# The low parts of the weights by a negated rounding on ScalarE and an accumulating DMA, in place of a subtraction on VectorE

## The chip, the cores and the metric

One NeuronCore of a Trainium2 chip. The metric is the device time of one execution in microseconds. The kernel before was run twice: 3788.08 and 3795.57 us, median 3791.82 us.

## The reference

The reference is the forward pass of a small network on 512 tokens of 1024 features in float32. First come two layers; each is a feed-forward block, a mixer and a second feed-forward block, every one followed by a layer norm (`LN(alpha*x + f(x))`). The mixer of the first layer ("even") joins a gated linear recurrence and an mLSTM, that of the second ("odd") an RWKV-7 delta rule and gated linear attention. Behind them stand two more layers with RMS norms, each with three kinds of attention (windowed, dilated, to a memory) merged by gates, and a feed-forward block with a short convolution.

```
def swiglu_ffn(x, wi, wo):
    gate, up = jnp.split(x @ wi, 2, axis=-1)
    return (jax.nn.silu(gate) * up) @ wo
```

Most of the work is products of the activations with weight matrices that are each used once: `wi` is 1024 x 5632, `wo` 2816 x 1024, and there are six such pairs beside the mixers' and attentions' matrices. All of it is float32, and the result must be close to float32.

## The kernel before, in words

Activations lie feature-major: eight tiles of 128 features x 512 tokens. A product in float32 is made of three faster passes in the format float32r, which holds fewer bits of the mantissa. Every operand is split in two, `hi` = the value rounded to float32r, and `lo` = value - hi, and a product is hi*hi + hi*lo + lo*hi (`mm3`, line 404).

Weights come as a stream of *slabs* in the order of their use (`plan_w`, line 331). A slab holds the columns of one output tile, 128 of them in most cases, and up to eight row tiles of 128 rows. On chip it is stored as *tiles* of 128 x 512 float32 (256 KB), four row tiles in each, so a full slab has two tiles. SyncE (SP) loads the raw tiles `wr` (`_dma`, line 336), as far as `raw_bufs` slabs ahead of the splitting. Then `_split_hi` (line 355) makes `wh` on ScalarE by a copy with rounding, and `_split_lo` (line 364) makes `wl` on VectorE as raw minus `wh`. `_split` (line 378) makes the low parts of one slab and the high parts of the next one, if there is room. TensorE reads `wh` twice and `wl` once for each row tile.

How far the splitting runs ahead is set when the program is written out. `slab` (line 389) takes the next slab, splits up to it if need be, and then splits `ahead` more (`split_ahead`, line 348), as long as no more than `hl_bufs` slabs are split and not used up. `gemm_first` (line 555), the first four output tiles after a norm, calls `split_ahead` four times more. `hl_bufs` is 8 for the first blocks, 2 with `raw_bufs` 1 in the odd mixer (HLB, RAWB, line 1129), 10, 4 and 7 in later ones. `ahead` is set by `man` (line 2640) at the start of every block: 1, but 2 for attention and 3 for the odd mixer. The constructor's value (line 239) holds only until the first of these calls. Raw, high and low tiles and most activations share one pool of 90 buffers (`f`, line 316); a buffer is taken again when its last reader is done.

The first four slabs, eight tiles, go another way: `load_start` (line 530) loads and splits them by halves of the features through `split_x`, with VectorE making the low part.

The order on each engine comes from three places. A small model in the kernel (`Sched`, line 71) prices every instruction and interleaves the main stream of products with background tasks (norms, mixers, attention); it notes a `dma_start` as landing 2500 ns after its start. A scheduler below it then orders the instructions of every engine by its own estimate and places the semaphores; in the attention blocks VectorE and ScalarE keep the order as written. After that each engine runs its queue in order and stops at an instruction whose operands are not there.

GpSimd (POOL) issues no DMA in this kernel. It has sums of squares and sums for the norms (`Stats.add`, line 594, and `RX.emit`, line 1933), a few products of the mixers and attentions, and memsets of the border columns of the convolution's tiles. A second loader is ScalarE's queue, for some masks, biases and the output.

Of the kernel before, what the change touches and what calls it, by code (L numbers as in the profile page):

```python
# [12 lines left out]
F32R = mybir.dt.float32r  # L13
AF = mybir.ActivationFunctionType
ALU = mybir.AluOpType
# [27 lines left out]
class Engine:  # L43
    """An engine whose instructions are noted with a rough price, for the order of emission."""
# [17 lines left out]
class Core:  # L62
    """The engines under their usual names."""
# [7 lines left out]
class Sched:  # L71
    """Interleaves emission: a main stream and background generators, by an estimate of when TensorE gets to an
    instruction and of when its operands are there. A generator yields a delay, At(time), a condition, or DONE:
    once all that it emitted in this step has run."""
# [6 lines left out]
    def __init__(self):  # L81
        self.t = 0.0
        self.eng = {"vector": 0.0, "scalar": 0.0, "gpsimd": 0.0, "sync": 0.0}
        self.ready, self.by = {}, {}
        # when the readers of a tile are done; the banks in use with the number of their last reader; free banks
        self.free, self.banks, self.idle, self.seq = {}, {}, [0.0] * 8, 0
        self.step_done = 0.0
        self.table = None
        # tasks: (time, number, rank, generator); of those that are due, the lowest rank goes first
        self.heap = []  # L90
        self.n = 0
        self.blocked = []
        self.busy = False
# [51 lines left out]
    def bank(self, ps):  # L145
        """A bank is taken."""
# [8 lines left out]
    def unbank(self, n):  # L155
        """The n banks read last are free."""
# [4 lines left out]
    def upto(self, *aps):  # L161
        """Runs what is due before these operands are there."""
# [63 lines left out]
class G:  # L226
    """What the parts of the kernel share: engines, pools, constants, the weight stream."""

    def __init__(self, ctx, tc, raw_bufs=3, hl_bufs=8, f_bufs=90, q_bufs=16):
# [9 lines left out]
        self.raw_bufs, self.hl_bufs, self.ahead = raw_bufs, hl_bufs, 1  # L239
        self.wq = []  # L240
        self.wi_dma = self.wi_hi = self.wi_split = self.wi_use = self.wi_done = 0
# [11 lines left out]
        # tri[j, i] = 1 where i >= j  # L253
# [10 lines left out]
    # -- TensorE  # L264
# [29 lines left out]
    def pace(self, engine="vector", lead=2000.0):  # L294
        """When that engine is about to run dry."""
# [5 lines left out]
    def acq(self, n):  # L301
        """For a background generator: waits until n banks are free."""
# [13 lines left out]
    def f(self, name, dt=F32, cols=NT):  # L316
        """A tile of up to 520 columns."""
# [5 lines left out]
    def load(self, dst, src):  # L323
        """A load that is not to start ahead of those emitted before it."""
        self.tc.keep_in_program_order(self.nc.sync.dma_start(dst, src))

    # -- the weight stream: slabs [128, kt, cols], in the order of use
# [3 lines left out]
    def plan_w(self, w, c0, cols, k0, kt):  # L331
        """w: DRAM [K, N]; rows 128*k0 .., kt row tiles."""
# [15 lines left out]
    def split_ahead(self, n=1):  # L348
        """Splits up to n more slabs, as far as there is room for them."""
# [5 lines left out]
    def _split_hi(self):  # L355
        parts = []
        for t in self.whl_t[self.wi_hi]:
            hi = self.f("wh", F32R, t.shape[1])
            self.nc.scalar.activation(hi, t, AF.Copy)
            parts.append((t, hi))  # L360
        self.whl_t[self.wi_hi] = parts
        self.wi_hi += 1

    def _split_lo(self):
# [3 lines left out]
        for raw, hi in self.whl_t[j]:  # L368
            lo = self.f("wl", F32R, raw.shape[1])
            self.nc.vector.tensor_tensor(lo, raw, hi, ALU.subtract)  # L370
# [7 lines left out]
    def _split(self):  # L378
        """The low parts of one slab; the high parts of the next one, if there is room."""
        if self.wi_hi == self.wi_split:  # L380
            self._split_hi()
        if self.wi_hi == self.wi_split + 1 and self.wi_hi < min(len(self.wq), self.wi_done + self.hl_bufs):
            self._split_lo()
            if self.wi_hi < self.wi_dma:
                self._split_hi()
        else:
            self._split_lo()

    def slab(self, ahead=None):
        """The next slab: a list of (hi, lo) by row tile."""  # L390
# [11 lines left out]
    # -- three passes of float32r: hi*hi + hi*lo + lo*hi  # L402
# [7 lines left out]
    def rsqrt(self, v, cols=NT):  # L410
        """1/sqrt(v): the table's value and one Newton step."""
# [9 lines left out]
    def preload(self, func):  # L421
        """Brings a function's table in ahead of its use."""
# [10 lines left out]
    def centred(self, ps, name):  # L433
        """ps [tokens, 4 heads of 128], each head less its mean."""
# [20 lines left out]
class Pipe:  # L455
    """Generators that advance by one stage at a time, the oldest first."""
# [7 lines left out]
    def add(self, gen):  # L464
        """One stage for all, then the first of the new one."""
# [9 lines left out]
class X:  # L475
    """Activations, feature-major: eight tiles [128 features, 512 tokens], each as hi + lo."""
# [10 lines left out]
def load_vectors(g, vecs):  # L487
    """vecs: name -> DRAM AP of n*128 values. Leaves each as columns [128, n] on chip."""
# [38 lines left out]
def load_start(g, x, X0, n=4):  # L527
    """x [512, 1024] to feature-major hi/lo, and the first n slabs, both by halves of the features."""
# [22 lines left out]
    g.wi_dma = g.wi_hi = g.wi_split = n  # L551
# [3 lines left out]
def gemm_first(g, xs, n, by_half=True):  # L555
    """The first n output tiles after a norm: the reduction outermost, by halves of the tokens."""
# [27 lines left out]
class Stats:  # L584
    """Sums over the features, per token."""
# [8 lines left out]
    def add(self, y, c=slice(0, NT), fast=False):  # L594
        """Adds one tile's columns c; fast: VectorE, not GpSimd."""
# [19 lines left out]
    def rstd(self, hf, eps):  # L615
        """Emits the mean (PSUM, all partitions) and 1/sqrt(var + eps) for one half."""
# [2088 lines left out]
```

## Time and profile before

| | |
|---|---|
| runs | 3788.08, 3795.57 us, median 3791.82 |
| profiled execution, span from the first to the last instruction | 3778.3 us, which is 13.5 us under the median of the runs; the time around the span is not given for this execution by itself |
| TensorE, matmul | 3718.2 us busy (98%), 19704 instructions |
| TensorE, weight load (beside the matmuls) | 3014.8 us (80%) |
| VectorE | 2083.9 us (55%) |
| ScalarE | 1472.4 us (39%) |
| GpSimd | 363.3 us (10%) |
| DMA | 331.83 MB, 88 GB/s on average; SP's queue keeps the 16 engines busy for 29.9% |
| mean granted TensorE clock | 0.989 of full speed |

Busy time is the time in which at least one instruction of the engine runs. A mean duration times a count can be more than it, since instructions of one engine overlap at their ends. A row of the waits names the waiting engine and its output, the engine and tile it waited for, the total, the number of waits and the longest. Line 55 is the helper that records each instruction and line 279 the one that issues matmuls, so rows are told apart by their tiles. The DMA share of a stretch is the mean busy share of the 16 DMA engines.

### The profile page before, as it was taken

The numbers are of one execution on the slowest core, as the hardware profiler recorded it, in microseconds if no ns is written. First come the engines' busy times: TensorE is split into PE (matmuls) and PEld (weight loads), VectorE is DVE, ScalarE is ACT, GpSimd is POOL, SyncE is SP. The second block draws the span as 40 slices with busy tenths as digits, with TensorE's granted clock in tenths as the row PEclk, the third lists the DMA queues.
The fourth block names the chain that finished last, engine by engine and source line by source line (L and its number), as shares of the span: only waits on it lengthen the run. The fifth ranks groups of instructions, "written<-read, shape, count | busy, mean of one in ns | idle before, by whom it ended". The sixth has DMA issues, their size and how long they took to land.

```text
span 3778.3 us, 52544 instructions
## 1 busy us (share of the span) xinstructions
PE 3718.2 (98%) x19704; PEld 3014.8 (80%) x19704; DVE 2083.9 (55%) x3891; ACT 1472.4 (39%) x2877; POOL 363.3 (10%) x571
## 2 busy tenths in 40 slices
PE   9999999999999999999999999999999999999999
PEld 7888878888888886677888877788888877788888
DVE  4334968333733378677432554558656745467655
ACT  4223664222422255533332433345334434344433
POOL 0001012000200020012000310022000210121001
PEclk9999999999999999889999999999999999999999
DMA  5332322333233311122333242232333242233331
GB/s 160 98 101 77 86 67 86 99 95 95 80 111 98 99 53 41 39 78 71 106 95 90 77 120 76 75 105 68 101 101 102 68 131 65 81 90 90 89 100 52
DMA packets 615090, 331.83 MB, mean 88 GB/s; under 512 B 25233, under 2 KB 608050, under 8 KB 614834
## 3 DMA queue, kind: packets, MB, share of 16 engines
q1 hardware_dynamic: 612018, 324.81, 29.9%
q10 hardware_dynamic: 2816, 3.64, 0.3%
q8 instruction: 155, 2.54, 0.3%
q14 instruction: 101, 0.83, 0.1%
HBM read 323.65 MB, written 4.74 MB: 87 GB/s over the span
## 4 chain that ended last, share of the span: by engine, by line
PE 90%; DVE 7%; ACT 1%; issue 1%; POOL 0%; DMA 0%; SPq 0%; ACTq 0%; DVEq 0%; POOLq 0%
PE m L279 62%; PE mg L279 5%; PE mh L279 3%; PE mf L279 3%; PE tk L279 3%; PE br L279 2%; DVE wl L55 1%; DVE ln_z L55 1%; DVE rm_t L55 1%; PE naS L279 1%; PE naO L279 1%; DVE x L55 1%; DVE xgl L55 1%; PE dO L279 1%; PE dS L279 1%
## 5 line engine op out<-in xcount | busy, mean ns | idle before, releaser
L55 DVE TENSOR_TENSOR wl<-wr,wh 128x512 fp32r<-128x512 f32 (+2 forms) x1208 | 814.9, 720 | 85.4 <-ACT wh L55 84.7
L55 ACT ACTIVATE wh<-wr 128x512 fp32r<-128x512 f32 (+2 forms) x1208 | 664.5, 606 | 93.2 <-PE m L279 50.5
L279 PE MATMUL m<-xh,wh 128*128 128x512 f32 x1544 | 619.3, 401 | 0.0
L279 PE MATMUL m<-xh,wl 128*128 128x512 f32 x1544 | 610.6, 395 | 0.0
L279 PE MATMUL m<-xl,wh 128*128 128x512 f32 x1544 | 610.2, 395 | 0.0
L279 PE MATMUL m<-xgh,wh 128*128 128x512 f32 x1184 | 475.5, 402 | 0.0
L279 PE MATMUL m<-xgl,wh 128*128 128x512 f32 x1184 | 467.6, 395 | 0.0
L279 PE MATMUL m<-xgh,wl 128*128 128x512 f32 x1184 | 467.2, 395 | 0.0
L55 DVE SCALAR_TENSOR_TENSOR hf<-sg,m 128x512 f32<-128x512 f32 x80 | 55.0, 688 | 575.2 <-PE m L279 565.9
L279 PEld LDWEIGHTS m<-xh,wh 128*128 128x128 f32 x1544 | 290.9, 188 | 74.4 <-issue 7.1
L279 PEld LDWEIGHTS m<-xh,wl 128*128 128x128 f32 x1544 | 291.0, 188 | 69.4 <-issue 0.7
L279 PEld LDWEIGHTS m<-xl,wh 128*128 128x128 f32 x1544 | 291.0, 188 | 67.6 <-issue 1.7
L279 PEld LDWEIGHTS m<-xgh,wh 128*128 128x128 f32 x1184 | 222.3, 188 | 62.8 <-issue 14.5
L279 PEld LDWEIGHTS m<-xgh,wl 128*128 128x128 f32 x1184 | 222.3, 188 | 52.3 <-issue 0.7
L279 PEld LDWEIGHTS m<-xgl,wh 128*128 128x128 f32 x1184 | 222.5, 188 | 49.4 <-issue 1.7
L279 PE MATMUL m<-hh,wh 128*128 128x512 f32 x600 | 236.4, 394 | 0.0
L279 PE MATMUL m<-hl,wh 128*128 128x512 f32 x600 | 236.3, 394 | 0.0
L279 PE MATMUL m<-hh,wl 128*128 128x512 f32 x600 | 236.2, 394 | 0.0
L55 ACT ACTIVATE sg<-m 128x512 f32<-128x512 f32 x80 | 47.8, 597 | 424.4 <-PE m L279 424.4
L55 ACT ACTIVATE hh<-hf 128x512 fp32r<-128x512 f32 x88 | 55.7, 633 | 382.6 <-DVE hf L55 382.6
L55 ACT ACTIVATE uc<-up,vecs 128x512 f32<-128x512 f32 x88 | 71.6, 816 | 203.0 <-DVE up L55 202.9
L55 DVE SCALAR_TENSOR_TENSOR uc<-up,vecs,uc 128x512 f32<-128x512 f32 x176 | 131.3, 748 | 13.2 <-ACT uc L55 7.0
(546 smaller groups left out, 6503.7 us busy)
## 6 DMA issues: line engine op xcount, KB each, us to landing
wr<-in_ffn_wi_dram SPq DMA_DIRECT2D x352, 256.0 KB
wr<-in_w_up_dram SPq DMA_DIRECT2D x176, 256.0 KB
wr<-in_ffn_wo_dram SPq DMA_DIRECT2D x160, 256.0 KB
wr<-in_w_in_dram SPq DMA_DIRECT2D x152, 256.0 KB
wr<-in_w_down_dram SPq DMA_DIRECT2D x80, 256.0 KB
wr<-in_od_w_in_dram SPq DMA_DIRECT2D x50, 256.0 KB
wr<-in_ev_w_in_dram SPq DMA_DIRECT2D x48, 256.0 KB
wr<-in_w_out_dram SPq DMA_DIRECT2D x32, 256.0 KB
```

Of the source, the lines that this page charges most:

```text
L55: r = fn(*a, **kw)
L279: return self.nc.tensor.matmul(out, lhsT, rhs, start=start, stop=stop, **kw)
```

## The change

The low part of a tile is no longer a subtraction on VectorE. ScalarE copies the raw tile with a scale of -1 into the low tile, which rounds it to float32r: it then holds minus the high part. A DMA issued by GpSimd adds the raw tile to it in place, from SBUF to SBUF, which leaves raw - hi. ScalarE then makes the high part as before. Both parts of one slab are made in one step, so the counter `wi_hi` and the look-ahead of the high parts go. The constructor's `ahead` becomes 2; `man` and `load_start`'s splitting stay. Comments and docstrings were taken out too; those lines are not shown.

```diff
-        self.raw_bufs, self.hl_bufs, self.ahead = raw_bufs, hl_bufs, 1
+        self.raw_bufs, self.hl_bufs, self.ahead = raw_bufs, hl_bufs, 2
...
-        self.wi_dma = self.wi_hi = self.wi_split = self.wi_use = self.wi_done = 0
+        self.wi_dma = self.wi_split = self.wi_use = self.wi_done = 0
...
-    def _split_hi(self):
-        parts = []
-        for t in self.whl_t[self.wi_hi]:
-            hi = self.f("wh", F32R, t.shape[1])
-            self.nc.scalar.activation(hi, t, AF.Copy)
-            parts.append((t, hi))
-        self.whl_t[self.wi_hi] = parts
-        self.wi_hi += 1
-
-    def _split_lo(self):
+    def _split(self):
         j = self.wi_split
         cols = self.wq[j][2]
         hl = []
-        for raw, hi in self.whl_t[j]:
-            lo = self.f("wl", F32R, raw.shape[1])
-            self.nc.vector.tensor_tensor(lo, raw, hi, ALU.subtract)
+        for raw in self.whl_t[j]:
+            hi, lo = self.f("wh", F32R, raw.shape[1]), self.f("wl", F32R, raw.shape[1])
+            self.nc.scalar.activation(lo, raw, AF.Copy, scale=-1.0)
+            self.nc.gpsimd.dma_start(lo, raw, accum_op=ALU.add)
+            self.nc.scalar.activation(hi, raw, AF.Copy)
             for k in range(lo.shape[1] // cols):
...
         self.wi_split += 1
         self._dma()
-    def _split(self):
-        if self.wi_hi == self.wi_split:
-            self._split_hi()
-        if self.wi_hi == self.wi_split + 1 and self.wi_hi < min(len(self.wq), self.wi_done + self.hl_bufs):
-            self._split_lo()
-            if self.wi_hi < self.wi_dma:
-                self._split_hi()
-        else:
-            self._split_lo()
...
-    g.wi_dma = g.wi_hi = g.wi_split = n
+    g.wi_dma = g.wi_split = n
```

## Rows read from the trace of the kernel before

**Rows 1.** The page, part 1: span, then busy time of each engine and its instructions.
```profile
span 3778.3 us, 52544 instructions
...
PE 3718.2 (98%) x19704; PEld 3014.8 (80%) x19704; DVE 2083.9 (55%) x3891; ACT 1472.4 (39%) x2877; POOL 363.3 (10%) x571
```
**Rows 2.** The page, part 4: the chain that ended last, share of the span by engine.
```profile
PE 90%; DVE 7%; ACT 1%; issue 1%; POOL 0%; DMA 0%; SPq 0%; ACTq 0%; DVEq 0%; POOLq 0%
```
**Rows 3.** Windows of two feed-forward stretches: length, busy (instructions) by engine, clock, DMA.
```profile
core 0: us, PE busy (x) PEld busy (x) DVE busy (x) ACT busy (x) POOL busy (x), PEclk, DMA share, GB/s
697.00:810.00 113.00, 113.00 (x489) 91.48 (x488) 39.05 (x64) 27.72 (x50) 0.00 (x0) 1.00 0.34 98
860.00:940.00 80.00, 80.00 (x347) 64.77 (x346) 25.89 (x42) 23.73 (x44) 0.00 (x0) 1.00 0.26 76
```
**Rows 4.** Waits of TensorE's matmuls over the span: us in total, times, longest.
```profile
PE mf L279 <- DVE xgl L55: 9.6, 10, 1.7
...
PE mk L279 <- DVE wl L55: 4.0, 2, 3.3
...
PE mv L279 <- DVE wl L55: 2.3, 1, 2.3
```
**Rows 5.** The page, part 5: the two groups that split weights; busy us, mean ns.
```profile
L55 DVE TENSOR_TENSOR wl<-wr,wh 128x512 fp32r<-128x512 f32 (+2 forms) x1208 | 814.9, 720 | 85.4 <-ACT wh L55 84.7
L55 ACT ACTIVATE wh<-wr 128x512 fp32r<-128x512 f32 (+2 forms) x1208 | 664.5, 606 | 93.2 <-PE m L279 50.5
```
**Rows 6.** Instructions that touch wl, 597 to 901.1 us: durations, first and last start.
```profile
L279 PEld LDWEIGHTS m<-xh,wl x257: 187/188/189, 644.4 to 900.5; 128*128 128x128 f32 x129
...
L55 DVE TENSOR_TENSOR wl<-wr,wh x112: 418/684/1785, 597.3 to 892.4; 128x512 fp32r<-128x512 f32 x104, 128x256 fp32r<-128x256 f32 x8
L279 PEld LDWEIGHTS m<-hh,wl x84: 187/188/189, 697.3 to 855.3; 128*128 128x128 f32 x84
...
L279 PEld LDWEIGHTS mf<-xh,wl x64: 187/188/193, 620.4 to 644.2; 128*128 128x128 f32 x64
```
**Rows 7.** Groups of TensorE's weight loads, 619.9 to 901.1 us: count, busy, mean.
```profile
L279 PEld LDWEIGHTS mg<-hh,wl 128*128 128x128 f32 x28 | 5.3, 188 | 1.2
```
**Rows 8.** Timeline of VectorE in the odd block: start, length, instruction.
```profile
1420.02 1.83 DVE L55 TENSOR_TENSOR wl<-wr,wh 128x512 fp32r<-128x512 f32 x2
```
**Rows 9.** The chain that ended last, 1380 to 1780 us: shares, pieces by start and length.
```profile
by line: PE m L279 21.8%; PE tk L279 5.6%; PE mh L279 3.9%; PE mv L279 3.6%; PE go L279 3.0%; PE oa L279 2.9%; DVE wl L55 2.8%; PE ob L279 2.6%; PE tV L279 2.5%; PE Z L279 2.1%; PE mf L279 2.0%; PE mk L279 2.0%; PE Y L279 1.9%; issue 1.9%; 
...
1423.32 2.79 PE tk L279 x12
...
1685.75 1.28 DVE wl L55 x2
```
**Rows 10.** Groups of VectorE, 697 to 810 us: the low parts made there.
```profile
L55 DVE TENSOR_TENSOR wl<-wr,wh 128x512 fp32r<-128x512 f32 x41 | 26.3, 685 | 0.0
...
L55 DVE TENSOR_TENSOR wl<-wr,wh 128x256 fp32r<-128x256 f32 x1 | 0.4, 420 | 0.0
```
**Rows 11.** Window at the start of the odd block, columns as in Rows 3.
```profile
1386.00:1460.00 74.00, 74.00 (x319) 53.35 (x318) 54.97 (x88) 54.16 (x112) 11.10 (x15) 1.00 0.21 61
```
**Rows 12.** Timelines of SP and of TensorE at the start: first load, first reader.
```profile
0.78 1.81 SPq L55 DMA_DIRECT2D xs<-in_x_dram  x4
...
3.82 1.02 PE L284 MATMUL xT<-ident,xs 128*128 128x128 f32 x2 [3.82 <-DMA xs<-in_x_dram]
```
**Rows 13.** Instructions that touch wr: SP's issues of loads, ns min/median/max.
```profile
L55 SPq DMA_DIRECT2D wr<-in_ffn_wi_dram x352: 367/368/1898, 2.6 to 2037.2; - x176
```
**Rows 14.** Groups of GpSimd over the span: count, busy us, mean ns, idle before.
```profile
L55 POOL TENSOR_TENSOR sq<-sq,sqh 128x256 f32<-128x256 f32 x56 | 53.6, 958 | 76.2 <-ACT sqh L55 74.5 <-PE mh L279 1.3
...
L55 POOL TENSOR_TENSOR sq<-sq,sqt 128x512 f32<-128x512 f32 x30 | 48.6, 1619 | 103.9 <-ACT sqt L55 103.9
```
**Rows 15.** DMA at the end, 3766 to 3778 us: packets, MB, share of engines.
```profile
q1 hardware_dynamic: 576, 1.05, 23.3%
```
**Rows 16.** DMA in the feed-forward stretch, 697 to 810 us: columns as before.
```profile
q1 hardware_dynamic: 22154, 11.00, 33.9%
```

## The prediction

> **What bounds the kernel now.** I read the page's shares first: TensorE is busy for 3718.2 of 3778.3 us [rows 1] and takes 90% of the chain that ended last [rows 2]. The reader is to see that only 3778.3 - 3718.2 = 60.1 us, 1.6%, are not TensorE's. The windows show the pace: in a stretch of gate and up products 347 matmuls fill 80 us at a granted clock of 1.00, one per 0.2305 us [rows 3], so a slab of 24 (eight row tiles, three passes) takes 5.53 us. The waits of TensorE say who is ever late: low parts of weights cost it 4.0 + 2.3 us, in two places, in the products of the memory's keys and values; the low part of the activations (xgl) costs 9.6 us [rows 4]. VectorE's work on low parts of weights is large, 1208 instructions and 814.9 us [rows 5], but is not what TensorE waits for.
>
> The next question is how far ahead a low part is made. Between 597 and 901.1 us VectorE makes 112 of them, 104 with four row tiles and 8 with two: 432 row tiles [rows 6]. They are those of the feed-forward block whose products start at 620.4. By 901.1 TensorE has used 64/2 (each weight twice, by halves) + 257 + 84 [rows 6] + 28 [rows 7] = 401. So 31 row tiles lie ready, and at 3 x 0.2305 us each that is 21 us of lead. In the odd block (1386 to 1777 us) at most two slabs may be split, and there the lead is gone: a pair of low parts ends at 1420.02 + 1.83 = 1421.85 [rows 8], the products that use it start at 1423.3, and low parts hold 2.8% of the chain's 400 us, some 11 us [rows 9].
>
> **The change, part by part.** The sums go against the profiled execution: a span of 3778.3 us, which is 13.5 us under the median of the runs (3791.8); I add the 13.5 at the end. The start's eight slab halves still go the old way, so 1200 tiles change.
>
> *VectorE loses* 814.9 x 1200/1208 = 810 us of busy time [rows 5]. TensorE waits for VectorE in few places, so the gain is bounded by the 9.6 us of xgl above; only a part of that stands behind weights, so I take -5, with 0 and -10 as ends.
>
> *ScalarE gains* the negated rounding: 1200 more of the instruction that makes the high part, 1208 of which take 664.5 us [rows 5], so about +660 us. It goes from 1472 [rows 1] to 2130 us of 3778. In the feed-forward stretch it is busy 27.7 of 113 us with 42 tiles [rows 3, 10], which becomes some 51. Hidden under TensorE there. In the odd block it is busy 54.2 of 74 us at the worst [rows 11], and each slab puts 1.1 us more into its queue ahead of evacuations and the solver's steps: I take +5 (0 to +15).
>
> *The high part moves*: it was made one slab before the low part, now in the same step, after the negation. It loses one slab of its lead and keeps the low part's 21 us. Cost nothing, covered by that lead.
>
> *The adding DMA.* Each has three prices. *Latency*: no row shows such a DMA; the nearest is the first load, issued at 0.78 and read at 3.82 [rows 12], 3.0 us. I take 4 us after the negation, since the issue lies on GpSimd, with 3 and 6 as ends, in place of VectorE's 0.7. In the feed-forward and attention blocks 4 goes into a lead of about 20 us and costs nothing; the raw tile is held some 3 us longer, which the same lead covers. In the odd block the low parts that come just in time move later by 3.3 us. Four to five slabs are exposed (those on the chain and those TensorE waited for [rows 4, 9]): 4.5 x 3.3 = +15 us, with 0 (the sequence hides it) and +40 (a dozen slabs) as ends.
>
> *Issue on GpSimd*: not shown; a load's issue on SP takes 0.37 us [rows 13], an add of 128x512 on GpSimd 1.6 us [rows 14]; these are the ends. I take 1.2 us, near the add since it is GpSimd's own work. There are 42 tiles in 113 us of the dense stretch [rows 10], one per 2.7 us, so it holds its rate. Behind the issue, which waits for ScalarE's negation, stand GpSimd's sums of squares and the border memsets. Sums stand on the way to the next norm: four boundaries of the second block with four or more issues between their adds, at 1.2 us each. Mostly they wait for ScalarE anyway, so +5 (0 to +20).
>
> *Transfer*: at the end of the kernel 512 packets of 2 KB (of 576; the other 64 are completions) take 23.3% of 16 engines for 12 us, 87 ns each [rows 15]. In the dense stretch loads take 33.9% [rows 16]; the same 11.00 MB in 2 KB packets, 5371 of them, cost 87 x 5371 / (16 x 113 us) = 26% per pass. An add that reads two operands and writes one may be one pass (26%), two (52%) or three (78%): 60%, 86% or 111% in total. I take two, because a copy's read and write fit in one pass [rows 15] and the add has one read more. At 86% the queue is busy but not the limit, and delays lie in the lead.
>
> The Trainium skill's page Collectives: The Full Stack, section The bandwidth ceiling: the fold count and why AG ≠ RS ≠ AR, says that an add in the DMA path runs at about half the rate of a copy, because it reads two sources (1.93 measured there). By it the sum would be 0.34 + 0.26 x 1.93 = 84%, the same verdict; three passes would come out against it. No row of the kernel before shows an adding DMA, so the trace neither agrees nor disagrees.
>
> *Two ahead*: the constructor's value is overwritten by the planning helper (1, 2 for attention, 3 for the odd block) before any slab is taken. Nothing.
>
> Sum: 3778.3 - 5 + 5 + 15 + 5 = 3798 of span, + 13.5 = **3812 us**, +0.5%. With all the ends, the likeliest case reaches from 3782 to 3867; I give it 3780 to 3865.
>
> **Rivals.** *The DMA engines become the limit (slower).* Place: the dense stretches; price: three passes or more. It decides from the point where 33.9% + n x 26% passes 100%, n = 2.55, a packet of 222 ns. At three passes, 111%, the six feed-forward blocks (about 370 us each, 2200 in all) stretch by 8 to 11%: +180 to +240, about 4020 us. At four (138%) it is +800, about 4600. For it: 86% is close, and 512 B loads and adds share the engines. Against: only 30% over the whole span, and 21 us of lead to level bursts. In the profile TensorE would wait for DMA into wl.
>
> *GpSimd becomes the limit (slower).* 363 us of own work [rows 1] + 1200 p exceeds the span at p = 2.85 us, and the dense stretch at 2.7. At p = 3.5 the kernel would take 363 + 4200 = 4563 us. For it: GpSimd's adds already run uneven, 958 ns on average at 128x256 where 128x512 takes 1619 [rows 14], so 1.2 times what its size would give; 1.6 x 1.2 is still only 1.9. No row shows such an issue, which is why both ends stay.
>
> *Every odd slab stalls (slower).* If all 34 slabs there wait 3.3 us, +112: 3905 us. Against: the block's long gaps of solver work fill most of them.
>
> *Faster.* All of TensorE's idle time gone would be 3718 + 13.5 = 3732, 1.6%; so faster by more than 2% needs products to run faster than 0.2305 us, and nothing here does that.
>
> *It does not do what it says*: for the look-ahead that is certain, at no cost; for the adds there is no such case.
>
> **How the numbers follow.** Chances: the forecast 0.58; DMA engines 0.15; GpSimd 0.15; odd block 0.08; something that saves over 2% 0.04. About 2% is what a measurement of this kernel tells from no change. So faster 0.04, within 2% 0.58, slower 0.38. Within 2% ends at 3868. For eight in ten the range takes in the forecast, the odd block, the three-pass case and part of GpSimd's: 3770 to 4300. The likeliest case's own range is 3780 to 3865.
>
> **What the profile after would show.** Right: VectorE near 1270 us, ScalarE near 2130, a GpSimd queue with 1200 x 128 packets that at two passes take 1200 x 128 x 174 ns / (16 x 3778 us) = 44% of the 16 engines, TensorE 97 to 98% busy, new waits for DMA into wl only between 1400 and 1780 us. Wrong: TensorE below 95% in 697 to 810 us, waits there for DMA into wl (DMA or GpSimd limit, told apart by the DMA share near 1.0 or GpSimd without idle time), or a packet over 222 ns. A time under 3760 would mean that VectorE's work held TensorE where the waits do not show it.

## The result and the profile after

The changed kernel takes 3835.9 us (median of 3835.72 and 3836.09) against 3791.8: a ratio of 1.0128, 95% interval [1.0088, 1.0168]. That is slower, but within 2%. Its profiled execution has a span of 3834.0 us, 55.7 more than that of before.

The page of the changed kernel, parts 1 to 3 (busy time and share of the span; in tenths by 40 slices the granted clock and the DMA engines; the DMA queues), answers to [rows 1]:

```profile
PE 3737.7 (97%) x19704; PEld 3038.2 (79%) x19704; DVE 1342.1 (35%) x2691; ACT 2063.4 (54%) x4076; POOL 1367.7 (36%) x1771
...
PEclk9999999999999999778999999999999999999999
DMA  9988666998899954237888866587998775798985
...
q0 software_dynamic: 172800, 304.90, 46.7%
q1 hardware_dynamic: 612018, 324.81, 30.2%
```

VectorE lost 742 us, ScalarE gained 591, GpSimd 1004. TensorE is still busy 97% of the span, but 19.5 us longer with the same 19704 matmuls, and its clock has a hole in slices 17 to 19, which is the odd block. The new queue q0 holds 16 engines for 46.7%.

The page of the changed kernel, parts 5 and 6: the new group of GpSimd (busy us, mean ns of one, idle before it and what ended it) and its transfers (KB each, median us from issue to landing):

```profile
L55 POOL DMA_DIRECT2D wl<-wr x1200 | 1058.0, 947 | 2033.7 <-ACT wl L55 1662.1
...
wl<-wr POOLq DMA_DIRECT2D x1110, 256.0 KB, 5.0
```

An issue costs GpSimd 0.95 us; it mostly stands idle and waits for the negation. An addition has landed 5.0 us after its issue, in the median.

Where are the 55.7 us? I take a block from the first product after one norm to the first after the next. Lengths in us, from the starts of the `mf` tiles in the two traces:

| block | before | after | difference |
|---|---|---|---|
| first feed-forward | 370.7 | 372.5 | +1.8 |
| even mixer | 233.9 | 240.3 | +6.4 |
| second and third feed-forward | 370.3, 370.7 | 373.4, 372.0 | +3.1, +1.3 |
| odd mixer | 416.4 | 450.6 | +34.2 |
| fourth feed-forward | 370.3 | 372.2 | +1.9 |
| attention, two | 428.8, 430.7 | 436.3, 436.4 | +7.5, +5.7 |
| feed-forward of the second part, two | 377.3, 393.7 | 375.3, 389.2 | -2.0, -4.5 |

The dense stretch first, since the expensive rivals stood there. The window of the changed kernel's second feed-forward block, at the same distance from the block's start as in [rows 3], and its DMA queues (columns as in [rows 3] and [rows 16]):

```profile
705.00:818.00 113.00, 113.00 (x489) 91.54 (x488) 15.17 (x22) 52.32 (x100) 36.75 (x43) 1.00 0.93 199
```

```profile
q0 software_dynamic: 6302, 11.07, 56.4%
q1 hardware_dynamic: 22807, 11.33, 36.2%
```

TensorE is busy all 113.00 us at full clock with the 489 matmuls of before, although the DMA share went from 0.34 to 0.93. Nothing is lost here.

The odd block as one window, of the kernel before (columns as in [rows 3]):

```profile
1361.20:1777.60 416.40, 400.78 (x3547) 305.05 (x3546) 301.31 (x636) 201.84 (x388) 46.71 (x57) 0.93 0.19 55
```

and of the changed kernel:

```profile
1373.90:1824.50 450.60, 419.72 (x3545) 320.84 (x3546) 254.00 (x560) 238.16 (x467) 111.07 (x138) 0.88 0.46 98
```

Two numbers are to be taken from each: TensorE's idle time is 416.40 - 400.78 = 15.6 before and 450.60 - 419.72 = 30.9 after, +15.3 us. Its busy time grew by 18.9 us for the same products, and the granted clock says why: 400.78 x 0.93 = 373 and 419.72 x 0.88 = 369 us at full clock, the same work within 1%. So the block's 34.2 us are 15.3 of waiting and 18.9 of lower clock. Who is waited for? The longest of TensorE's waits in that window of the changed kernel (us in total, times, longest):

```profile
PE m L279 <- DMA wl<-wr: 3.7, 2, 2.0
PE st L279 <- DVE sq L55: 3.4, 1, 3.4
PE mv L279 <- DMA wl<-wr: 3.2, 1, 3.2
PE gA L279 <- DVE gAT L55: 3.0, 1, 3.0
PE S L279 <- DVE M L55: 3.0, 2, 2.7
PE oa L279 <- DVE yl L55: 2.5, 1, 2.5
```

Low parts of weights: 3.7 + 3.2 = 6.9 us, against 4.0 + 2.3 = 6.3 before [rows 4]. They did not become the problem. Here an addition lands 4.2 us after its issue, in the median (transfers of the block, KB each, median us):

```profile
wl<-wr POOLq DMA_DIRECT2D x82, 256.0 KB, 4.2
```

The other tiles that VectorE hands over (steps of the solver, of the output, sums) are waited for 19.4 us, against 6.8 before. One of these waits, the 3.0 us for `gAT`, can be followed back. `gAT` stands in VectorE's queue behind an instruction on `yl` that takes 0.68 us in the kernel before and 10.5 us here, while GpSimd runs eight additions one behind the other (start, length; GpSimd, then VectorE):

```profile
1633.05 10.19 POOL L55 TENSOR_TENSOR y<-xh,xl 128x512 f32<-128x512 f32 x8
```

```profile
1633.27 10.54 DVE L55 TENSOR_TENSOR yl<-yvr,yh 128x512 fp32r<-128x512 f32 x1 [3.48 <-ACT yh L55]
```

In the kernel before, the same eight additions are there, and every VectorE instruction beside them gets through in at most 1.8 us:

```profile
1608.03 11.63 POOL L55 TENSOR_TENSOR y<-xh,xl 128x512 f32<-128x512 f32 x8 [3.39 <-PE R L279]
```

So in the changed kernel VectorE is held up beside GpSimd's additions until the last of them is done; the experiments show it again.

In the attention blocks a wait is new. TensorE's waits of the changed kernel in the first of them, and SP's issues of the value windows over the whole span (ns min/median/max):

```profile
PE naO L279 <- DMA Vw<-va: 4.5, 3, 1.6
```

```profile
L55 SPq DMA_DIRECT2D Vw<-va x16: 629/1205/3907, 2274.4 to 3104.0; - x16
```

Before, the same sixteen issues:

```profile
L55 SPq DMA_DIRECT2D Vw<-va x16: 607/653/2182, 2219.9 to 3037.4; - x16
```

### The profile page after: what moved, and what is told of

Its sections match the earlier page's. It is cut to its first block, busy times and chain, and to the rows that moved or that the text cites. A ratio compares the mean times of both kernels' runs of the same rounds, so it can differ in the third digit from the quotient of the medians.

```text
span 3834.0 us, 55639 instructions
## 1 busy us (share of the span) xinstructions
PE 3737.7 (97%) x19704; PEld 3038.2 (79%) x19704; DVE 1342.1 (35%) x2691; ACT 2063.4 (54%) x4076; POOL 1367.7 (36%) x1771
## 3 DMA queue, kind: packets, MB, share of 16 engines
q0 software_dynamic: 172800, 304.90, 46.7%
## 4 chain that ended last, share of the span: by engine, by line
PE 86%; DVE 5%; issue 3%; DMA 3%; ACT 2%; POOL 1%; SPq 0%; DVEq 0%; POOLq 0%; ACTq 0%
PE m L279 59%; PE mg L279 5%; PE mh L279 4%; PE mf L279 4%; PE tk L279 3%; PE br L279 2%; DMA Vw<-va 1%; DMA wl<-wr 1%; DVE ln_z L55 1%; PE naS L279 1%; PE naO L279 1%; DVE rst L55 1%; PE dO L279 1%; PE dS L279 1%; POOL wl L55 1%
## 5 line engine op out<-in xcount | busy, mean ns | idle before, releaser
L55 POOL DMA_DIRECT2D wl<-wr x1200 | 1058.0, 947 | 2033.7 <-ACT wl L55 1662.1
L55 ACT ACTIVATE wl<-wr 128x512 fp32r<-128x512 f32 (+2 forms) x1200 | 726.8, 606 | 58.4 <-DMA wr<-in_ffn_wi_dram 28.6
L55 ACT ACTIVATE wh<-wr 128x512 fp32r<-128x512 f32 (+2 forms) x1208 | 730.2, 605 | 20.6 <-DMA wl<-wr 15.1
```

The lines of the kernel that those rows point to most:

```text
L55: r = fn(*a, **kw)
```

## The experiments

In all of them a weight tile's way is chosen by its block: `sub` is the split of before, `add` that of the change. The common edit, then one line for each kernel:

```diff
+MODE = {...}                       # way by block, "*" for all others
+        self.blk_of.append(self.blk)     # in plan
...
+        mode = MODE.get(self.blk_of[j], MODE["*"])   # in _split_hi and _split_lo
```

**Which block?** First the odd block back to the subtraction, the rest as changed:

```diff
+MODE = {"*": "add", "odd": "sub"}
```

> The odd block takes 450.6 us in the changed kernel and 416.4 us before, 34.2 of the 55.7 us that the span grew by. Here the 83 weight tiles of that block are split as before (high part a slab ahead, low part subtracted by VectorE), all others by the adding DMA. Theory A, waiting for the low part: the odd block splits at most two slabs ahead, so the 5.0 us (median) until an addition has landed stand where VectorE took 0.7 us; the block returns to about 416 us and the kernel takes 3836 - 34 = 3802 us. Theory B, load: the additions cost time by what they keep busy (ScalarE, GpSimd, DMA engines), wherever they stand; the block has 83 of 1200 tiles, so it gives back about 56 x 83 / 1200 = 4 us, and the kernel takes 3832 us.

3797.9 us, ratio to before 1.0036 [1.0015, 1.0058]. Its odd block:

```profile
1372.20:1784.20 412.00, 394.66 (x3546) 300.16 (x3546) 290.28 (x626) 205.71 (x396) 49.90 (x64) 0.94 0.23 61
```

Theory B (load, evenly) falls: 83 of 1200 tiles hold 0.92 of the 1.28%. Why they do, this run does not tell, since it undoes every part of the change there.

```diff
+MODE = {"*": "sub", "odd": "add"}
```

> The reverse: the adding DMA in the odd block alone (83 tiles), the subtraction on VectorE everywhere else. Theory A (the wait in a block with two slabs of look-ahead): the odd block is as long as in the changed kernel, about 450 us, and the kernel takes 3792 + 34 = 3826 us. Theory B (load, shared by all tiles): 3792 + 4 = 3796 us.

3805.9 us, 1.0064 [1.0039, 1.0088], between the two forecasts: about 22 us over the 3783.8 of the kernel before beside it. The odd block:

```profile
1362.80:1798.60 435.80, 408.18 (x3545) 309.61 (x3546) 264.71 (x568) 234.11 (x459) 106.63 (x130) 0.91 0.45 97
```

TensorE's instructions of the block stand in the changed kernel's order but for a few, yet it is 14.8 us shorter: 11.5 at a better clock, 3.3 of idle time (27.6 against 30.9).

**The transfer, or ScalarE's part?**

```diff
+MODE = {"*": "add", "odd": "addv"}
...
+                if mode == "addv":
+                    self.nc.vector.tensor_tensor(lo, raw, lo, ALU.add)   # for the DMA
```

> In the odd block alone the negated rounding stays on ScalarE, but VectorE adds the raw tile to it in place of the DMA; all other tiles by the adding DMA. ScalarE has the same work and the high part comes equally late as in the changed kernel; only the DMA's issue and its time to landing are gone. Theory A (time to landing): the odd block comes back to 416 to 422 us, the kernel takes 3802 to 3808 us. Theory C (83 negations of 0.62 us in ScalarE's queue, 51 us, and the high part made a slab later, delay the solver's steps): the block stays near 450 us, the kernel at 3830 to 3836 us.

3823.6 us, 1.0100 [1.0067, 1.0132]. The odd block:

```profile
1374.50:1805.00 430.50, 400.11 (x3545) 307.69 (x3546) 296.45 (x635) 241.09 (x469) 50.02 (x57) 0.90 0.21 57
```

Without one adding DMA in the block, TensorE's idle time is 430.50 - 400.11 = 30.4 us, that of the changed kernel. This is what theory C expected of the idle time; the block is shorter than it expected by the clock. TensorE waits 14.0 us for tiles of ScalarE (2.4 before) and 17.7 for tiles of VectorE (13.1 before), in this execution longest for

```profile
PE oa L281 <- ACT yh L56: 7.0, 1, 7.0
```

This wait does not show a crowded ScalarE. ScalarE itself had just been idle, waiting for VectorE:

```profile
1718.20 0.63 ACT L56 ACTIVATE rs<-gvr 128x512 f32<-128x512 f32 x1 [3.60 <-DVE gvr L56]
```

So the landing time is not needed for the loss: what is left of the change here, ScalarE's second copy, the later high part and a new order, is enough for it. Which of the three it is, this run does not tell.

**Work that nobody waits for.**

```diff
+MODE = {"*": "add", "odd": "shadow"}
...
+                if mode == "shadow":       # after the subtraction
+                    sh = self.f("shw", F32R, n)
+                    self.nc.scalar.activation(sh, raw, AF.Copy, scale=-1.0)
+                    self.nc.gpsimd.dma_start(sh, raw, accum_op=ALU.add)
```

> In the odd block VectorE subtracts as before and TensorE reads that; beside it every tile is also negated by ScalarE into a spare tile to which GpSimd's DMA adds the raw tile, and which nothing reads. So the block has all the work of the changed kernel (83 negations, 83 issues, 21 MB of additions) but TensorE waits for none of it. Theory A (the wait): 416 to 422 us for the block, 3802 to 3810 us for the kernel. Theory B or C (the work itself, on the DMA engines, GpSimd or ScalarE): the block stays near 450 us, the kernel at 3830 to 3840 us.

3888.6 us, 1.0254 [1.0217, 1.0290], more than any theory said. The odd block:

```profile
1373.20:1876.60 503.40, 449.61 (x3546) 338.94 (x3545) 292.96 (x635) 241.89 (x469) 116.09 (x140) 0.80 0.42 89
```

This was a poor experiment: the interleaving model is told of the extra work, too, and by the two traces only about half of TensorE's sequence of products is alike to that of before (1 is the same sequence; the changed kernel's is 0.5 to 0.6 alike, by how one counts). But it raised the right question, whether the order alone costs time. The next three tell the model one thing and run another, `.real` being the engine without the model:

```diff
+MODE = {"*": "sub", "odd": "add_told"}
...
+                self.s.note("vector", "tensor_tensor", (lo, raw, hi, ALU.subtract), {})
+                self.nc.scalar.real.activation(lo, raw, AF.Copy, scale=-1.0)
+                self.nc.gpsimd.real.dma_start(lo, raw, accum_op=ALU.add)
+                self.nc.scalar.real.activation(hi, raw, AF.Copy)
```

> The adding DMA in the odd block alone, with all its instructions, but the model that interleaves the work while the program is written (Sched) is told the old split: a high part on ScalarE a slab ahead and a subtraction on VectorE. TensorE's instructions of the block then stand nearly in the order of the kernel before (0.97 alike, against 0.54 for the adding DMA in the odd block with its own prices). Theory D, order: the model's prices for the new split (two ScalarE copies and a transfer of 2500 ns) moved the products against the solver's steps, and that costs the time; with the old order the block takes 416 to 422 us and the kernel 3784 to 3790 us. Theory A, the wait for the addition to land: the block stays near 436 us, the kernel near 3806 us.

3804.1 us, 1.0049 [1.0033, 1.0066]. The odd block:

```profile
1364.00:1792.10 428.10, 402.11 (x3545) 305.83 (x3545) 263.64 (x561) 239.38 (x462) 108.84 (x132) 0.93 0.46 99
```

The clock is that of before, the idle time 26.0 us. The kernel's time is what theory A said, the block's length stands between the two theories. But TensorE waits only 7.8 us for low parts of weights; its longest wait is for a step of the solver on VectorE:

```profile
PE M L281 <- DVE KG L56: 6.8, 1, 6.8
```

```diff
+MODE = {"*": "sub", "odd": "sub_told"}
...
+                self.s.note("scalar", "activation", (lo, raw, AF.Copy), {})
+                self.s.note("gpsimd", "dma_start", (lo, raw), {})
+                self.s.note("scalar", "activation", (hi, raw, AF.Copy), {})
+                self.nc.scalar.real.activation(hi, raw, AF.Copy)
+                self.nc.vector.real.tensor_tensor(lo, raw, hi, ALU.subtract)
```

> The other half of the pair: in the odd block the high part on ScalarE and the subtraction on VectorE, no addition by DMA, but the model is told the prices of the new split, so that TensorE's instructions stand nearly in the order of the changed kernel (0.96 alike; 0.55 against before). Theory D (order): the block takes about 436 us without any adding DMA, the kernel about 3804 us. Theory A (the wait): 412 to 418 us for the block, 3780 to 3788 us for the kernel.

3803.6 us, 1.0043 [1.0028, 1.0058]. The odd block:

```profile
1363.50:1788.80 425.30, 402.02 (x3545) 306.77 (x3546) 304.91 (x643) 196.15 (x384) 46.82 (x49) 0.92 0.19 53
```

Idle 23.3 us with no addition and no second copy on ScalarE. The new order, together with the high part that is no longer a slab ahead, costs time by itself. The kernel's time is that of theory D; the block is 11 us shorter than D said. This run does not tell the order from the late high part.

```diff
+MODE = {"*": "sub", "odd": "shadow_told"}    # e4's spare work by .real, not told
```

> The block's subtraction on VectorE as before, and beside it 83 negations on ScalarE into spare tiles and 83 additions by DMA that nothing reads, none of them told to the model: the order is that of before (0.98 alike) and nobody waits for an addition, but all its work is there. The same work told to the model gave a block of 503 us. Theory D: 416 to 424 us for the block, 3784 to 3792 us for the kernel; the 503 were the order. Theory B or C (the work itself): 450 us or more, 3815 us or more.

3797.5 us, 1.0032 [1.0015, 1.0049], above what D allowed, far below the 503 us of the run that told the model. The odd block, and its longest wait:

```profile
1364.60:1789.00 424.40, 399.73 (x3547) 303.47 (x3546) 308.55 (x636) 240.25 (x463) 110.28 (x132) 0.92 0.46 101
```

```profile
PE mk L281 <- DVE wl L56: 10.0, 2, 9.3
```

Idle 24.7 us in nearly the order of before, and nobody waits for an addition. VectorE's own low part is late instead, and not for want of the high part, which ScalarE had made by 1614.5 us. The subtraction itself is held up, beside the same eight additions of GpSimd as in the changed kernel (VectorE, then GpSimd):

```profile
1618.48 10.48 DVE L56 TENSOR_TENSOR wl<-wr,wh 128x512 fp32r<-128x512 f32 x2
```

```profile
1617.40 10.39 POOL L56 TENSOR_TENSOR y<-xh,xl 128x512 f32<-128x512 f32 x8
```

The first of these two subtractions takes 9.9 us. The 6.8 us of e5 have the same cause: a VectorE instruction of 128x256 that takes 10.3 us there, 0.4 in the kernel before, ahead of `KG`. Six of the kernels have all the additions by DMA in the odd block, and five of them (the changed one, e2, e5, e7 and e8 below) show such an instruction of 9.9 to 10.5 us beside the eight; the sixth, e4, and the eight kernels without these additions in the block have none above 1.8 us. So it goes with GpSimd's issues; why VectorE does not get in between the eight additions is not shown.

The single executions' idle times, against 15.6 to 17.3 in the order of before: work alone +8, work and waiting (e5) +9 to +10, order and late high part alone +7, all of it 27.6 to 30.9, +11 to +15. Without the one wait behind the eight additions, e7 has 24.7 - 9.3 = 15.4 us, no more than before, and e5 26.0 - 6.8 = 19.2. So the work costs through this one collision, as far as this run shows, and an estimate of the wait for the landing, from the difference of the two, is some 4 us.

**Is it the order, over the whole kernel?**

```diff
+MODE = {"*": "add_told"}
```

> All 1200 tiles by the adding DMA, in every block, with the model told the old split everywhere, so the order on TensorE is near that of before. Theory D: the odd block, the even one and the attentions come back to their lengths of before (416, 234, 429 and 431 us), the second feed-forward blocks keep what they gained (2 + 4.5 us), the first ones their 1 to 3 us each: 3784 + 8 - 6.5, so 3780 to 3795 us. Theory A: the waits stay, 3825 to 3836 us as in the changed kernel.

3828.8 us, 1.0123 [1.0101, 1.0146]: no measurable gain over the changed kernel's 1.0128. The odd block:

```profile
1379.20:1809.30 430.10, 399.79 (x3546) 303.27 (x3545) 254.01 (x553) 242.97 (x471) 113.20 (x140) 0.93 0.48 104
```

Here the old order gives the old clock, 0.93, but the idle time stays at 30.3 us, and the even block (242.8) and the attentions (439.3, 438.6) are no shorter than in the changed kernel. Of the 30.3 us, 6.8 are the same wait behind GpSimd's eight additions as in e5. Theory D is not the cause of the whole: the order, with the late high part, can cost 7 us of idle time (e6), but the order of before brought none of it back here.

**How near was the DMA limit?**

```diff
+MODE = {"*": "sub", "f1": "twice", "f2": "twice", "f3": "twice", "f4": "twice"}
...
+                        self.nc.gpsimd.dma_start(lo, self.zero[:, 0:n], accum_op=ALU.add)
```

> How much room do the DMA engines have? In the four feed-forward blocks of the first two layers every low tile gets a second adding DMA, which adds a tile of zeros (one buffer of the shared pool less, 89); all other blocks subtract on VectorE. In the changed kernel's dense stretch loads take 36% and additions 56% of the 16 engines, 93% in all, with TensorE busy all the time. Theory L (the busy share is a limit): 0.36 + 2 x 0.56 = 1.48, so the blocks stretch from 372 to some 550 us each and the kernel to about 3784 + 4 x 175 = 4490 us, TensorE waiting for DMA into wl. Theory N (the share contains waiting inside the engines and has room above 93%): the blocks stay at 372 to 390 us, the kernel under 3860 us.

4425.3 us, 1.1681 [1.1647, 1.1715]: within 2% of theory L's 4490, so theory N falls. In 120:240 us, the first block, window, queues and waits of TensorE:

```profile
120.00:240.00 120.00, 98.61 (x376) 75.33 (x375) 14.28 (x26) 38.84 (x72) 60.39 (x71) 0.91 1.10 213
```

```profile
q0 software_dynamic: 9610, 16.57, 82.0%
q1 hardware_dynamic: 18520, 8.91, 27.5%
```

```profile
PE m L283 <- DMA wl<-zero: 21.3, 9, 4.4
```

376 matmuls in 120 us, 0.319 us each, where the dense stretch of the changed kernel had 489 in 113, 0.231: 1.38 times. The blocks took 518 to 542 us. The DMA share stands at 1.10; above 1 it counts packets of the two queues that overlap in time on an engine. But the DMA engines are not shown to be the limit. The second issue of a tile waits in GpSimd's queue for the first addition to land:

```profile
POOL wl L56 <- DMA wl<-wr: 56.2, 26, 6.5
```

With its 60.4 us of work that is 116.6 of the 120 us, so GpSimd's queue is as full as the DMA engines. That the landing takes 6.4 us in the median here, where it took 4.7 in the changed kernel's dense stretch, speaks for crowded engines, too. The two limits were not separated.

**The attentions.**

```diff
+MODE = {"*": "sub", "attn": "shadow_told"}
```

> The two attention blocks are 7.6 and 5.7 us longer in the changed kernel. Here they subtract on VectorE as before, and beside it every tile is negated into a spare tile and added to by DMA, which nothing reads and the model is not told; all other blocks as before. Theory B' (work: the additions crowd the other transfers, since SP's issue of the value windows Vw went from 0.66 to 1.28 us in the median and TensorE waits 4.5 and 3.8 us for them): both blocks 5 to 8 us longer, the kernel at 3792 to 3798 us. Theory A (the wait for the low parts of the weights): no more than 2 us longer, 3782 to 3786 us.

3804.1 us, 1.0045 [1.0027, 1.0062]; in its profiled execution the two blocks took 438.7 and 438.9 us, 9.9 and 8.2 more than before, although nothing waits for an addition. TensorE waits for the value windows:

```profile
PE naO L281 <- DMA Vw<-va: 10.4, 6, 3.5
```

That speaks for theory B', the work. The spare tiles also take buffers of the shared pool, which the change does not, so the size is an upper bound. The real additions there:

```diff
+MODE = {"*": "sub", "attn": "add"}
```

> The adding DMA in the two attention blocks alone, with the model's own prices; all other blocks subtract. If the blocks' loss is their own (as in the odd block's case), they take 436 us each, 13 us more together, and the kernel 3795 us. If it came over from the blocks around them (slabs and transfers at the boundaries), they stay within 3 us of before and the kernel at 3782 to 3788 us. Against the run with the spare tiles it tells the wait (this one longer) from the work (both alike).

3790.2 us, 1.0014 [0.9997, 1.0031]; blocks of 433.1 and 430.5 us, 4.1 more than before together. That is shorter than with the spare tiles, so the wait for an addition is not shown as the larger part (TensorE waits 4.9 us for low parts there). The wait for Vw is there:

```profile
PE naO L281 <- DMA Vw<-va: 8.3, 5, 2.9
```

By themselves the two blocks cost at most 0.3%. Their windows, in this kernel,

```profile
2146.80:2580.00 433.20, 419.13 (x2163) 335.24 (x2164) 155.86 (x412) 233.41 (x528) 159.85 (x178) 0.98 0.69 153
2959.00:3389.50 430.50, 416.63 (x2162) 332.36 (x2161) 156.84 (x409) 226.98 (x514) 162.20 (x180) 0.99 0.70 158
```

in the changed one,

```profile
2196.70:2633.00 436.30, 420.58 (x2163) 335.61 (x2164) 150.97 (x406) 236.15 (x534) 164.89 (x184) 0.98 0.71 155
3008.30:3444.80 436.50, 421.54 (x2162) 334.91 (x2162) 154.24 (x406) 230.84 (x522) 166.70 (x186) 0.98 0.71 158
```

and in the one before:

```profile
2147.90:2576.60 428.70, 420.88 (x2164) 333.38 (x2163) 226.16 (x523) 175.31 (x409) 61.93 (x65) 1.00 0.31 91
2953.90:3384.70 430.80, 423.32 (x2163) 334.56 (x2162) 231.02 (x522) 170.36 (x396) 61.70 (x64) 0.99 0.31 90
```

TensorE's idle time is 14.1 and 13.9 us here, 15.7 and 15.0 in the changed kernel, 7.8 and 7.5 before. So most of the new waiting is the blocks' own, that for the value windows included (8.3 us here, 8.4 in the changed kernel). The lengths differ by the busy time: 8.4 us less than before here, 2.1 less in the changed kernel. Its order of products is new in both, so idle time and busy time cannot be held against each other one by one. Why the two blocks are 13.2 us longer when the blocks around them add as well, and only 4.1 by themselves, stays open.

**A version that beats both.** VectorE has its relief where it has most else to do, in the convolution and norms of the second part:

```diff
+MODE = {"*": "sub", "ff": "add"}
```

> The adding DMA in the two feed-forward blocks of the second part alone, where VectorE's steps of the convolution and the norms stand beside the splitting; everything else subtracts as before. In the changed kernel these blocks took 375.3 and 389.2 us, before 377.3 and 393.7. If that gain is VectorE's relief (theory V), the kernel takes 3782 - 6.5 = 3775 us, 0.2% under before. If it was scatter between executions (theory S): 3782 to 3786 us.

3776.1 us (12 runs) against 3788.1 beside it, 0.9976 [0.9961, 0.9992]: faster, as theory V said, but by less than the quarter of a percent that the medians give. The runs of both kernels spread with the mean granted clock. At a clock of 0.985 three runs of this kernel average 3789.5 us and twelve of before 3794.4; at 0.989 and 0.990 eight average 3774.8 and seven of before 3778.1. So it gains 3 to 5 us at the same clock; the rest is that more of its runs had the better one. In its profiled execution the two blocks take 375.9 and 392.4 us, 1.4 and 1.3 less than before.

**How much of the odd block is scatter.** The run before, e1, and the last three with only other blocks changed (e10, e11, e12) have TensorE's instructions of the odd block in the same order. Three windows, of the kernel with the addition in the second part's feed-forward blocks (e11),

```profile
1360.80:1788.40 427.60, 411.45 (x3546) 312.61 (x3545) 300.92 (x636) 202.03 (x388) 46.48 (x57) 0.90 0.19 54
```

of the one with the addition in the attentions (e12),

```profile
1361.30:1774.80 413.50, 397.28 (x3547) 302.21 (x3546) 300.91 (x636) 202.10 (x388) 46.53 (x57) 0.94 0.19 56
```

and of the one with the spare additions there (e10):

```profile
1359.10:1783.70 424.60, 408.41 (x3547) 311.08 (x3547) 301.01 (x636) 202.06 (x388) 46.48 (x57) 0.91 0.19 54
```

The idle time is 16.2 us in all three; the lengths differ by 14 us through the clock alone (0.90 to 0.94). So lengths of this block from single executions tell nothing below some 15 us, and idle times do. That is why the comparisons above go by idle time and, for the time, by the ratios.

## Why the prediction was right, and where its steps failed

The verdict held (no change within 2%), and so did the range; the forecast of 3812 us was 24 too low. A part of that is luck. The span was to be 3798 and is 3834.0, 36 over. The 13.5 us that I put outside the span were no such thing: the changed kernel has 1.7 us there (3835.72 - 3834.0), so one error hid a third of the other. And the range held through room that I had given to late low parts and to GpSimd's sums, which took next to none of it. The profiled execution of before will have been one of the shorter ones: the kernel before gave 3773 to 3799 us in the later runs, with medians of 3782, 3784 and 3788.

- *The odd block* (+15 for late low parts, +5 for ScalarE) is the step that failed, in its cause more than in its size. TensorE's waits for low parts grew from 6.3 to 6.9 us, not by 15. The latency is about what I assumed (4.2 us from the issue in this block, for 4 after the negation), but most of it lies in the look-ahead: the runs put its cost between 0.5 us (idle time of the changed kernel against e3) and some 4 us (e5 against e7, an estimate). The idle time did grow by 15.3 us, and e3 has all of it without a DMA, so it comes from steps that I priced at 5 or at nothing: ScalarE's second copy, the high part's lost lead, the order. I had called the lost slab of lead nothing, covered by 21 us; that lead exists in the feed-forward blocks, not in the odd one. The new order on TensorE follows from the model's prices; with the late high part it costs 7 us by itself (e6), and I had not counted it at all. Nor had I counted that VectorE is held up beside GpSimd's eight additions: 3.0 us in the changed kernel, 6.8 and 9.3 in e5 and e7. What the second copy costs alone, no run shows.
- *The clock* was missing: 18.9 us. The sum took a product at one pace everywhere. In the odd block the granted clock averages 0.93, and fell to 0.88. How much of it is the change's is open. The program of before itself shows busy times of 394.7 to 411.5 us there, and e2, in the changed kernel's order, 408.2. But not all of it is scatter: both runs of the changed kernel have a mean clock of 0.979 over the whole span, the 74 later runs of before 0.984 to 0.991.
- *The dense stretch* was right: TensorE at 113.00 of 113 us, DMA share 0.93 against 0.86. A packet takes 46.7% x 16 x 3834.0 us / 153,600 = 187 ns (I took 174), under the 222 from which the engines would limit. The Trainium skill, page Collectives: The Full Stack, section The bandwidth ceiling: the fold count and why AG ≠ RS ≠ AR, has a collective that adds at about half the rate of one that copies (1.93). This trace agrees in kind and has it slower: 187 / 87 = 2.1. The rival of three passes did not come. With a second addition per tile (e9) the blocks stretched by 39 to 45%; whether the DMA engines did that, as in this rival, or GpSimd's queue, as in the next, is not separated.
- *GpSimd* issues in 0.95 us (1.2 assumed), far from the 2.85 of that rival; its queue holds 46.7% (44% forecast). Its sums did not delay the second part, where the feed-forward blocks gained 6.5 us. The -5 for VectorE has the right sign and size there, and e11 confirms the sign, with 3 to 5 us. Its place was only in part the one I gave: TensorE's waits for xgl in these blocks fell from 3.3 us to nothing, but over the whole kernel they stayed (9.6 before, 9.7 after).
- *Not in the sum*: +8.1 in the first four feed-forward blocks and +6.4 in the even one, where TensorE waits 3.6 us for a low part, which I had excluded outside the odd block; and +13.2 in the attentions, where TensorE waits 8.4 us for the value windows, whose loads the additions delay, and 4.4 for low parts. These waits are not the whole account, since e12 has them, too (8.3 and 4.9), with blocks only 4.1 us longer. Over the whole span the waits for low parts of weights went from 6.3 to 15.0 us. I had looked at loads of weights only, for which the lead covers a delay.

So of 55.7 us: 34.2 odd, 13.2 attentions, 6.4 even, 8.1 and -6.5 feed-forward, 0.3 around them. In the odd block, the split between ScalarE's copy, the late high part, the order and the hold-up beside GpSimd's additions is not settled by the runs: the order and the late high part come together in e6, and the pieces don't add up exactly.

## What to carry to other kernels

An edit to a side stream also moves every instruction that a planner places by its prices; compare the order of the bound engine before looking for waits, and hold the order fixed when a cost is to be measured by itself. A lead measured in one stage covers nothing in another: where the look-ahead is two slabs, ask which engine each step is moved to and what stands in its queue. A wait row names the tile that came last, not why it was late: look at the length of the instruction that made it, and at what the other engines did beside it. And in stages with gaps, split every difference into idle time and busy time at the granted clock, because the same program scatters there by more than the effect.

## What the runs showed that was not expected

An addition by DMA within SBUF costs 187 ns per packet (2 KB, in some tiles less) where the copy to the output took 87 [rows 15], and in the dense stretch, with 93% of the engines' time taken, TensorE lost nothing. SP's other transfers feel the crowd: its issue of a value window (186 KB) went from 653 to 1205 ns in the median. A VectorE instruction that takes 0.4 to 0.7 us elsewhere took 9.9 to 10.5 us beside eight additions of GpSimd, in five of the six kernels that issue all the odd block's additions from GpSimd. And the granted clock of one and the same order of instructions in the odd block averaged 0.90 to 0.94 in five kernels, which made 394.7 to 411.5 us of busy time out of the same products.
